# Transposed input in its own buffers, first weight blocks in halves, and the memory prepared earlier and partly on GpSimd, in a two-layer hybrid encoder

## The chip, the core and the metric

The kernel runs on one core of one Trainium2 chip. The metric is the device time of one execution in microseconds (us), the median of several runs. A core has TensorE (PE in the profile; its weight loads are PEld), VectorE (DVE), ScalarE (ACT), GpSimd (POOL) and SyncE (SP), which here only issues transfers. Each engine takes its instructions in a fixed order.

## What is computed

`DEPTH` = 2 layers act on `x` (256 frames of 1024 numbers, float32), with a memory `mem` of 256 rows of 1024:

```python
for l in range(DEPTH):
    h = rms_norm(x, ffn1_norms[l, 0])
    x = x + 0.5 * rms_norm(swiglu(h, ffn1_w13[l], ffn1_w2[l]), ffn1_norms[l, 1])
    h = rms_norm(x, mix_norms[l, 0])
    x = x + rms_norm(token_mixing(h, ...), mix_norms[l, 1])     # retention, latent attention, differential attention, gated and summed
    h = rms_norm(x, cross_norms[l, 0])
    m = rms_norm(mem, cross_norms[l, 2])
    x = x + rms_norm(cross_attention(h, m, cross_wq[l], cross_wkv[l], cross_wo[l]), cross_norms[l, 1])
    h = rms_norm(x, ffn2_norms[l, 0])
    x = x + 0.5 * rms_norm(swiglu(h, ffn2_w13[l], ffn2_w2[l]), ffn2_norms[l, 1])
```

## The kernel before

**Products in three passes.** Each float32 operand of a large product is split into a high part (written in the matmul format by ACT) and a low part (the rest, by DVE); a product is three matmuls, high by high, high by low and low by high. A weight block is [128 x 1024] float32 (512 KB). `load` brings it into one of 4 `raw` buffers with a transfer on SP's queue, then `split` writes `wh` (ACT, L170) and `wl` (DVE, L171), of which there are 8 each. A block serves both halves `i` of the 256 frames, 12 matmuls in all.

**The start.** While the first data come in, 14 matmuls on zeros run (L145). `first_chunk` then computes four weight blocks against the transposed input. Its piece (half `i` of the frames, half `h` of the 1024 rows) is loaded into a work buffer `xg` (two buffers in turn, L253, on SP's queue), multiplied by a gain (DVE, L254) and split into `xTh` and `xTl`. The first two weight blocks are loaded and split in halves, the others whole. The plain `x` and its mean squares follow.

**The mixer of a layer.** Three token mixers run one after the other; `weave` takes one step of each of its generators in turn, so that projections and gates (`fill`) stand between the short, dependent steps of attention. The last attention is `differential`: scores, softmax (DVE L892, L559, ACT L561, DVE L898 to L902), transposes on PE (L910), values (L920), and a norm of each head through POOL (L923, L680, L682, L156, L157, L925) and DVE (L927). Then `branches(2, ...)` and the output projection follow, in `finish`.

**The memory.** `memory` loads the transposed memory `mT` in two pieces into `raw` buffers, and makes of each of its 8 rows of tiles a scaled high part (ACT, L173) and low part (DVE, L174) in `mem`; it is woven with `branches(2, ...)`. In layer 0 it also loads the plain memory `m` in two pieces into `raw` buffers, for the mean square (ACT, L164) and the reciprocal root (POOL), kept in `rmem` (L954) for both layers. `cross` reads `mem` and `rmem`.

**Order.** The program is written in Python order, and a scheduler at compile time places each instruction in the queue of its engine; an instruction that comes late in the program can stand earlier in its queue where its engine has nothing else. So the transfer of `positions`, which the program names after 22 weight blocks, is issued behind the ninth block. `rope_tables`, called in the first feed-forward of layer 0 after its second chunk, makes the tables of the rotations.

Of the kernel before, what the change touches and what calls it, by code (L numbers as in the profile page):

```python
# [11 lines left out]
F32 = mybir.dt.float32  # L12
# [3 lines left out]
AF = mybir.ActivationFunctionType  # L16
ALU = mybir.AluOpType
# [3 lines left out]
P = 128  # L21
D = 1024
KD = D // P
SEQ = 256
NT = SEQ // P
# [86 lines left out]
def hybrid_encoder(ctx: ExitStack, tc: tile.TileContext, stream: Stream, t: dict, out: bass.AP):  # L112
    nc = tc.nc
# [3 lines left out]
    wp = ctx.enter_context(tc.tile_pool(name="wp", bufs=WP_BUFS))  # L117
# [35 lines left out]
    def rsq(ss, n=1, eps=EPS, c=1.0):  # L153

        a, b = stat(n), stat(n)
        nc.gpsimd.tensor_scalar(out=a, in0=ss, scalar1=eps, scalar2=c, op0=ALU.add, op1=ALU.mult)  # L156
        nc.gpsimd.tensor_tensor(out=b, in0=a, in1=mhalf[:, :n], op=ALU.pow)  # L157
        return b
# [8 lines left out]
    def split(h, l, src, scale=None):  # L167

        if scale is None:
            nc.scalar.activation(h, src, AF.Copy)  # L170
            nc.vector.tensor_tensor(out=l, in0=src, in1=h.bitcast(F32), op=ALU.subtract)  # L171
        else:
            nc.scalar.activation(h, src, AF.Copy, scale=scale)  # L173
            nc.vector.scalar_tensor_tensor(out=l, in0=src, scalar=scale, in1=h.bitcast(F32), op0=ALU.mult, op1=ALU.subtract)  # L174

    def load(blk, parts=1):

        blk = _freeze(blk)
        w = _blk_width(blk)
        off = stream.place(blk)  # L180
        raw = wp.tile([P, w], F32, tag="raw", name="raw", padded_shape=[P, BLK])
        h = hp.tile([P, w], F32R, tag="wh", name="wh", padded_shape=[P, BLK])
        l = hp.tile([P, w], F32R, tag="wl", name="wl", padded_shape=[P, BLK])
        for n in range(parts):
            c = slice(n * w // parts, (n + 1) * w // parts)
            nc.sync.dma_start(out=raw[:, c], in_=ws[off:off + P * w].rearrange("(p e) -> p e", p=P)[:, c])
            split(h[:, c], l[:, c], raw[:, c])
        nk = blk[3]
        return (h.rearrange("p (k n) -> p k n", k=nk), l.rearrange("p (k n) -> p k n", k=nk))
# [13 lines left out]
    def weave(*gens, fill=None):  # L203

        gens = list(gens)
        while gens:
            if fill is not None:
                next(fill, None)
            gens = [g for g in gens if next(g, gens) is not gens]
# [34 lines left out]
            nc.tensor.matmul(o, lhsT=aT[1][:, j0 + k, :], rhs=bh, start=False, stop=j0 + k == total - 1)  # L244
        tick()

    def first_chunk(blks, use):

        def scaled(i, h):

            k = slice(4 * h, 4 * h + 4)
            xg = wk.tile([P, 4, P], F32, tag="xg", name="xg")
            nc.sync.dma_start(out=xg, in_=t["xT"][:, i, k, :])  # L253
            nc.vector.tensor_tensor(out=xg, in0=xg, in1=gain0[:, k].unsqueeze(2).to_broadcast([P, 4, P]), op=ALU.mult)  # L254
            split(xT[i][0][:, k, :], xT[i][1][:, k, :], xg)

        def low(n):
            for i in range(NT):
                for k in range(2):
                    nc.tensor.matmul(o[i], lhsT=xT[i][1][:, 2 * n + k, :], rhs=tiles[n][0][:, k, :], start=False, stop=n == len(blks) - 1 and k == 1)  # L260

        o, tiles, r = [ps_tile() for _ in range(NT)], [], []
        for n, blk in enumerate(blks):
            if n % 2 == 0:
                scaled(0, n // 2)
            tiles.append(load(blk, 2 if n < 2 else 1))
            if n % 2 == 0:
                scaled(1, n // 2)
            for i in range(NT):
                for k in range(2):  # L270
                    mm2(o[i], xT[i][0][:, 2 * n + k, :], tiles[n][0][:, k, :], tiles[n][1][:, k, :], n == 0 and k == 0)
            if n:
                low(n - 1)
        for i in range(NT):
            nc.sync.dma_start(out=x[i], in_=t["x"][i * P:(i + 1) * P, :])
            r.append(rsq(mean_sq(x[i], D)))
        nc.sync.dma_start(out=ident, in_=t["c_ident"])
        low(len(blks) - 1)
        tick()
        for i in range(NT):  # L280
            use(i, o[i], r[i])
        return r
# [122 lines left out]
    def ffn(f, l, r, pg, ng, beside=lambda: None):  # L405
        b = _ffn_blocks(f, l)
        with tc.tile_pool(name="ff", bufs=2) as ff:
# [38 lines left out]

            first = r is None
            if first:
                r = first_chunk(b["w13", 0], both)
            else:  # L450
                lead(b["w13", 0], lambda i, o: both(i, o, r[i]), b["g", 1], use_gate(1))
            accs = new_accs()
# [26 lines left out]

    cs = const.tile([P, NT, 2, ROPE_W], F32, name="cs")  # L480

    def rope_tables():
        with tc.tile_pool(name="rt", bufs=1) as rt:
            n = ROPE_W // 2
            pi = rt.tile([P, NT], I32, name="pi")
            nc.sync.dma_start(out=pi, in_=t["positions"].rearrange("(t p) -> p t", p=P), allow_slow_non_contiguous=True)
# [84 lines left out]
    def mixer(l, r, pg, ng):  # L571
        with ExitStack() as es:
# [93 lines left out]
            def branches(b, y):  # L666
                return chain(branch(b, 0, y), branch(b, 1, y))
# [207 lines left out]
            def differential():  # L875
                steps = []
                for i in range(NT):
                    c = {}
                    steps += [[lambda i=i, c=c, g=g, fn=fn: fn(i, c, g) for fn in (dscores, dprobs, dvalues)] for g in range(2)]
                    steps[-1].append(lambda i=i, c=c: into_T(y_diff[i], 0, c["y"], 4))  # L880
                yield from skew(steps)
# [45 lines left out]
                    nc.vector.tensor_tensor(out=heads(c["y"], P), in0=heads(op, P), in1=f2.unsqueeze(2).to_broadcast([P, DIFF_H, P]), op=ALU.mult)  # L927

            mem = [xp.tile([P, KD, SEQ], F32R, tag=f"big{n}", name="mem") for n in range(2)]
            weave(differential(), fill=fill)  # L930
            weave(chain(fill, branches(2, y_diff)), memory(l, mem))

            work = [(xT, n, k) for n, k in enumerate(_rows("w_out", (l,), 8))]
            return finish(new_accs(), work, pg, ng, 1.0, True), mem
# [2 lines left out]
    def memory(l, mem):  # L937

        g = stat(KD)
        nc.sync.dma_start(out=g, in_=t["mgain"][l])  # L940
        for h in range(2):
            m = wp.tile([P, 4, SEQ], F32, tag="raw", name="mT")
            nc.sync.dma_start(out=m, in_=t["memT"][:, 4 * h:4 * h + 4, :])
            for k in range(4):
                mh, ml = (d[:, 4 * h + k, :] for d in mem)
                gk = g[:, 4 * h + k:4 * h + k + 1]
                split(mh, ml, m[:, k, :], gk)
                if k % 2:
                    yield
        if l == 0:  # L950
            for i in range(NT):
                m = wp.tile([P, D], F32, tag="raw", name="m")
                nc.sync.dma_start(out=m, in_=t["mem"][i * P:(i + 1) * P, :])
                nc.gpsimd.tensor_copy(out=rmem[:, i:i + 1], in_=rsq(mean_sq(m, D)))  # L954

    def cross(l, r, mem, pg, ng):
        with ExitStack() as es:
            cp = es.enter_context(tc.tile_pool(name="cp", bufs=2))
# [71 lines left out]
    r = None  # L1030
    for l in range(DEPTH):
        g = {k: t[f"{k}_norms"][l] for k in ("ffn1", "mix", "cross", "ffn2")}
        r = ffn("ffn1", l, r, g["ffn1"][1], g["mix"][0], *((rope_tables,) if l == 0 else ()))
        r, mem = mixer(l, r, g["mix"][1], g["cross"][0])
        r = cross(l, r, mem, g["cross"][1], g["ffn2"][0])
        r = ffn("ffn2", l, r, g["ffn2"][1], t["ffn1_norms"][l + 1, 0] if l + 1 < DEPTH else None)
# [64 lines left out]
```

## Time and profile before

| | us |
|---|---|
| median of 3 runs | 1456.21 (1455.73 to 1457.08) |
| the profiled execution, its own time | 1453.58 |
| span of its instructions | 1451.8 |
| PE busy | 1432.7 |
| DVE busy | 921.8 |
| ACT busy | 754.7 |
| POOL busy | 90.8 |

The span runs from the first to the last instruction of the profiled execution; its own time is 1.8 us longer. Busy time is the time in which an engine had at least one instruction under way. PE's share is 99%, so any change can win only where PE waits or runs at a lower clock. In the timeline a row gives start, length, engine, line, operation, output and inputs, count, and in brackets the idle time before it and what ended it; an engine with a q is its queue issuing a transfer.

### The profile page before, as it was taken

The numbers are of one execution on the slowest core, as the hardware profiler recorded it, in microseconds if no ns is written. First come the engines' busy times: TensorE is split into PE (matmuls) and PEld (weight loads), VectorE is DVE, ScalarE is ACT, GpSimd is POOL, SyncE is SP. The second block draws the span as 40 slices with busy tenths as digits, with TensorE's granted clock in tenths as the row PEclk, the third lists the DMA queues.
The fourth block names the chain that finished last, engine by engine and source line by source line (L and its number), as shares of the span: only waits on it lengthen the run. The fifth ranks groups of instructions, "written<-read, shape, count | busy, mean of one in ns | idle before, by whom it ended". The sixth has DMA issues, their size and how long they took to land.

```text
span 1451.8 us, 18502 instructions
## 1 busy us (share of the span) xinstructions
PE 1432.7 (99%) x6778; PEld 1189.6 (82%) x6778; DVE 921.8 (63%) x1209; ACT 754.7 (52%) x1102; POOL 90.8 (6%) x190
## 2 busy tenths in 40 slices
PE   8999999999999999999999999999999999999998
PEld 6888888888778888888888888888887788888886
DVE  5776576566767556665576555865667765665554
ACT  5444455654556646454464544666555565554442
POOL 0000022100201001000000000221001010000000
PEclk9999999999999999999999999999999999999999
DMA  8777756454466437777577765655444574476672
GB/s 277 245 259 262 241 183 207 153 160 141 154 201 217 155 127 229 257 237 232 190 224 246 249 227 199 208 175 186 145 155 145 163 239 145 140 258 226 218 227 92
DMA packets 109020, 290.14 MB, mean 200 GB/s; under 512 B 14909, under 2 KB 38397, under 8 KB 108925
## 3 DMA queue, kind: packets, MB, share of 16 engines
q1 hardware_dynamic: 76528, 265.89, 55.9%
q10 hardware_dynamic: 32400, 23.08, 4.9%
q8 instruction: 53, 0.87, 0.3%
q14 instruction: 39, 0.31, 0.1%
HBM read 276.34 MB, written 12.58 MB: 199 GB/s over the span
## 4 chain that ended last, share of the span: by engine, by line
PE 80%; DMA 8%; DVE 5%; ACT 3%; issue 2%; POOL 1%; SPq 0%; ACTq 0%; DVEq 0%; POOLq 0%
PE ps L226 25%; PE ps L227 25%; PE ps L231 24%; DMA gM<-far 4%; PE ps L312 2%; DMA raw<-in_ws 2%; DMA far<-gB 2%; DVE wl L171 2%; ACT wh L170 1%; PE ps L835 1%; PE ps L855 1%; PE ps L244 1%; POOL st L157 0%; DVE tg L657 0%; ACT junk L344 0%
## 5 line engine op out<-in xcount | busy, mean ns | idle before, releaser
L171 DVE TENSOR_TENSOR wl<-raw,wh 128x1024 fp32r<-128x1024 f32 (+1 forms) x480 | 575.0, 1213 | 206.7 <-ACT wh L170 198.1
L170 ACT ACTIVATE wh<-raw 128x1024 fp32r<-128x1024 f32 (+1 forms) x480 | 498.5, 1050 | 285.8 <-PE ps L231 185.0
L226 PE MATMUL ps<-wh,xTh 128*128 128x512 f32 (+1 forms) x1312 | 518.3, 395 | 4.9 <-ACT xTh L170 2.7
L227 PE MATMUL ps<-wl,xTh 128*128 128x512 f32 (+1 forms) x1312 | 510.6, 389 | 1.9 <-DVE wl L171 1.8
L231 PE MATMUL ps<-wh,xTl 128*128 128x512 f32 (+1 forms) x1256 | 488.9, 390 | 1.0 <-DVE xTl L174 0.9
L226 PEld LDWEIGHTS ps<-wh,xTh 128*128 128x128 f32 x1312 | 246.7, 188 | 57.9 <-ACT xTh L170 5.3
L227 PEld LDWEIGHTS ps<-wl,xTh 128*128 128x128 f32 x1312 | 246.9, 188 | 52.0 <-DVE wl L171 4.2
L231 PEld LDWEIGHTS ps<-wh,xTl 128*128 128x128 f32 x1256 | 235.8, 188 | 50.9 <-DVE xTl L174 1.8
L226 PE MATMUL ps<-wh,gTh 128*128 128x512 f32 x352 | 137.2, 390 | 0.0
L231 PE MATMUL ps<-wh,gTl 128*128 128x512 f32 x352 | 137.0, 389 | 0.0
L227 PE MATMUL ps<-wl,gTh 128*128 128x512 f32 x352 | 136.9, 389 | 0.0
L170 ACT ACTIVATE gTh<-gM 128x512 fp32r<-128x512 f32 (+1 forms) x48 | 28.6, 597 | 156.1 <-DMA gM<-far 156.1
L171 DVE TENSOR_TENSOR gTl<-gM,gTh 128x512 fp32r<-128x512 f32 (+1 forms) x48 | 31.0, 646 | 105.5 <-ACT gTh L170 105.5
L231 PEld LDWEIGHTS ps<-wh,gTl 128*128 128x128 f32 x352 | 66.1, 188 | 13.8
L227 PEld LDWEIGHTS ps<-wl,gTh 128*128 128x128 f32 x352 | 66.1, 188 | 13.7
L226 PEld LDWEIGHTS ps<-wh,gTh 128*128 128x128 f32 x352 | 66.1, 188 | 13.5
L350 POOL TENSOR_SCALAR st<-st 128x1 f32<-128x1 f32 x16 | 4.9, 306 | 941.2 <-ACT junk L344 941.2
L432 DVE SCALAR_TENSOR_TENSOR g<-ps,st,s 128x512 f32<-128x512 f32 (+1 forms) x48 | 33.7, 703 | 28.4 <-PE ps L231 28.4
L561 ACT ACTIVATE e<-ps,st 128x256 f32<-128x256 f32 (+1 forms) x80 | 33.6, 431 | 34.4 <-DVE st L559 34.3
L226 PE MATMUL ps<-wh,mem 128*128 128x512 f32 x128 | 51.0, 398 | 0.0
L231 PE MATMUL ps<-wh,mem 128*128 128x512 f32 x128 | 50.0, 390 | 0.0
L227 PE MATMUL ps<-wl,mem 128*128 128x512 f32 x128 | 49.9, 390 | 0.0
(203 smaller groups left out, 1279.2 us busy)
## 6 DMA issues: line engine op xcount, KB each, us to landing
raw<-in_ws SPq DMA_DIRECT2D x464, 512.0 KB, 4.5
far<-gB ACTq DMA_DIRECT2D x40, 256.0 KB, 2.3
gM<-far ACTq DMA_DIRECT2D x40, 256.0 KB, 4.6
gain<-in_ffn_norms SPq DMA_DIRECT2D x7, 512.0 KB, 5.4
raw<-in_ws SPq DMA_DIRECT2D x8, 416.0 KB, 5.2
gain<-in_mix_norms SPq DMA_DIRECT2D x4, 512.0 KB, 5.2
gain<-in_cross_norms SPq DMA_DIRECT2D x4, 512.0 KB, 5.3
mT<-in_memT SPq DMA_DIRECT2D x4, 512.0 KB, 3.5
```

The source lines that it names most:

```text
L170: nc.scalar.activation(h, src, AF.Copy)
L171: nc.vector.tensor_tensor(out=l, in0=src, in1=h.bitcast(F32), op=ALU.subtract)
L226: nc.tensor.matmul(o, lhsT=ah, rhs=bh, start=first, stop=False)
L227: nc.tensor.matmul(o, lhsT=ah, rhs=bl, start=False, stop=False)
L231: nc.tensor.matmul(o, lhsT=al, rhs=bh, start=False, stop=last)
L244: nc.tensor.matmul(o, lhsT=aT[1][:, j0 + k, :], rhs=bh, start=False, stop=j0 + k == total - 1)
L312: nc.tensor.transpose(p[:rows, i * P:(i + 1) * P], src[:, i * rows:(i + 1) * rows], ident)
L350: nc.gpsimd.tensor_scalar(out=a, in0=parts[0], scalar1=parts[1], scalar2=EPS * c, op0=ALU.add, op1=ALU.add)
L432: nc.vector.scalar_tensor_tensor(out=g[:, :w], in0=up, scalar=r, in1=s[:, :w], op0=ALU.mult, op1=ALU.mult)
L561: nc.scalar.activation(e[:, h, :w], s[:, j, :], AF.Exp, bias=nm[:, h:h + 1], accum_out=sums[:, h:h + 1])
L835: nc.tensor.matmul(s[h], lhsT=qT[i][:, 4 * g + h, :], rhs=kT[:, 4 * g + h, :w], start=True, stop=True)
L855: nc.tensor.matmul(op[:, cc], lhsT=c["pT", g][:, k, h * P:(h + 1) * P], rhs=mv[k][:, 4 * g + h, :], start=k == 0, stop=k == i)
```

## The change

Four edits. (1) The pieces of the transposed input get four buffers of their own, and their transfers are issued on ACT's queue, all at the start. (2) All four blocks of `first_chunk` are loaded and split in halves. (3) `memory` is woven with `differential` instead of with `branches(2, ...)`; the scaling and the subtraction go to POOL, and ACT makes a plain copy. (4) The mean squares of `mem` move out of `memory` into `rope_tables` (now `tables`), that is into the first feed-forward of layer 0, with a buffer of their own, one for both pieces.

```diff
-    def first_chunk(blks, use):
+    def first_chunk(blks, use, pool):
+
+        xs = [[pool.tile([P, 4, P], F32, name=f"xs{i}{h}") for h in range(2)] for i in range(NT)]
+        for h in range(2):
+            for i in range(NT):
+                nc.scalar.dma_start(out=xs[i][h], in_=t["xT"][:, i, 4 * h:4 * h + 4, :])
 
         def scaled(i, h):
 
             k = slice(4 * h, 4 * h + 4)
-            xg = wk.tile([P, 4, P], F32, tag="xg", name="xg")
-            nc.sync.dma_start(out=xg, in_=t["xT"][:, i, k, :])
+            xg = xs[i][h]
             nc.vector.tensor_tensor(out=xg, in0=xg, in1=gain0[:, k].unsqueeze(2).to_broadcast([P, 4, P]), op=ALU.mult)
             split(xT[i][0][:, k, :], xT[i][1][:, k, :], xg)
...
-            tiles.append(load(blk, 2 if n < 2 else 1))
+            tiles.append(load(blk, 2))
...
             if first:
-                r = first_chunk(b["w13", 0], both)
+                with tc.tile_pool(name="first", bufs=1) as pool:
+                    r = first_chunk(b["w13", 0], both, pool)
...
-    def rope_tables():
+    def tables():
+
         with tc.tile_pool(name="rt", bufs=1) as rt:
+            for i in range(NT):
+                m = rt.tile([P, D], F32, name="m")
+                nc.sync.dma_start(out=m, in_=t["mem"][i * P:(i + 1) * P, :])
+                nc.gpsimd.tensor_copy(out=rmem[:, i:i + 1], in_=rsq(mean_sq(m, D)))
             n = ROPE_W // 2
...
-            weave(differential(), fill=fill)
-            weave(chain(fill, branches(2, y_diff)), memory(l, mem))
+            weave(differential(), memory(l, mem), fill=fill)
+            weave(chain(fill, branches(2, y_diff)))
...
                 gk = g[:, 4 * h + k:4 * h + k + 1]
-                split(mh, ml, m[:, k, :], gk)
+                nc.gpsimd.tensor_scalar(out=m[:, k, :], in0=m[:, k, :], scalar1=gk, scalar2=None, op0=ALU.mult)
+                nc.scalar.activation(mh, m[:, k, :], AF.Copy)
+                nc.gpsimd.tensor_tensor(out=ml, in0=m[:, k, :], in1=mh.bitcast(F32), op=ALU.subtract)
                 if k % 2:
                     yield
-        if l == 0:
-            for i in range(NT):
-                m = wp.tile([P, D], F32, tag="raw", name="m")
-                nc.sync.dma_start(out=m, in_=t["mem"][i * P:(i + 1) * P, :])
-                nc.gpsimd.tensor_copy(out=rmem[:, i:i + 1], in_=rsq(mean_sq(m, D)))
...
-        r = ffn("ffn1", l, r, g["ffn1"][1], g["mix"][0], *((rope_tables,) if l == 0 else ()))
+        r = ffn("ffn1", l, r, g["ffn1"][1], g["mix"][0], *((tables,) if l == 0 else ()))
```

## Rows read from the trace of the kernel before

**Rows 1.** The page, busy time, share of the span and instructions of each engine.

```profile
PE 1432.7 (99%) x6778; PEld 1189.6 (82%) x6778; DVE 921.8 (63%) x1209; ACT 754.7 (52%) x1102; POOL 90.8 (6%) x190
```

**Rows 2.** Busy time by stretch: length, engines (instructions), granted clock, DMA share, GB/s.

```profile
7.00:23.00 16.00, 13.14 (x52) 9.16 (x51) 10.23 (x14) 9.51 (x16) 1.50 (x4) 1.00 0.84 305
34.00:40.00 6.00, 5.69 (x24) 4.10 (x23) 4.39 (x6) 5.67 (x8) 0.00 (x0) 1.00 0.58 194
410.00:415.00 5.00, 4.45 (x21) 3.13 (x20) 5.00 (x7) 3.76 (x5) 0.00 (x0) 1.00 0.68 218
415.00:420.00 5.00, 3.31 (x13) 2.16 (x13) 5.00 (x8) 2.51 (x3) 0.00 (x0) 0.92 0.66 213
420.00:425.00 5.00, 5.00 (x20) 3.90 (x20) 3.30 (x5) 1.55 (x2) 0.00 (x0) 0.74 0.79 260
1135.00:1140.00 5.00, 4.10 (x20) 3.07 (x20) 4.29 (x7) 1.66 (x2) 0.00 (x0) 1.00 0.64 198
```

**Rows 3.** Timeline of the start.

```profile
0.72 0.39 SPq L253 DMA_DIRECT2D xg<-in_xT  x1
1.16 1.28 ACT L140 ACT_TABLE_LOAD   x1 [1.16 <-PEq L1074]
4.84 0.69 DVE L254 TENSOR_TENSOR xg<-xg,st 128x512 f32<-128x512 f32 x1 [3.35 <-DMA st<-in_gain]
6.94 0.33 SPq L253 DMA_DIRECT2D xg<-in_xT  x1
6.95 0.40 PE L226 MATMUL ps<-wh,xTh 128*128 128x512 f32 x1
20.53 1.98 PE L260 MATMUL ps<-wh,xTl 128*128 128x512 f32 x8
22.34 0.62 PE L226 MATMUL ps<-wh,xTh 128*128 128x512 f32 x2
```

**Rows 4.** Tile xg in the first 40 us, its transfers' time from issue to landing.

```profile
DMA to landing us min/median/max: 3.9/4.3/4.7
```

**Rows 5.** Timeline of ACT from 386 us, where it turns from weights to the memory.

```profile
392.49 1.06 ACT L170 ACTIVATE wh<-raw 128x1024 fp32r<-128x1024 f32 x1 [0.40 <-DMA raw<-in_ws]
396.63 1.06 ACT L164 ACTIVATE junk<-m 128x1024 bf16<-128x1024 f32 x1 [3.08 <-DMA m<-in_mem]
402.97 1.05 ACT L170 ACTIVATE wh<-raw 128x1024 fp32r<-128x1024 f32 x1
```

**Rows 6.** Timeline of SP's queue in the same stretch.

```profile
388.85 0.33 SPq L186 DMA_DIRECT2D raw<-in_ws  x1
397.80 13.56 SPq L186 DMA_DIRECT2D raw<-in_ws  x7
```

**Rows 7.** Tile mT: ns min/median/max, first and last start in us, forms.

```profile
L173 ACT ACTIVATE mem<-mT,st x16: 493/501/509, 397.7 to 1119.2; 128x256 fp32r<-128x256 f32 x16
L174 DVE SCALAR_TENSOR_TENSOR mem<-mT,st,mem x16: 476/480/485, 398.2 to 1119.9; 128x256 fp32r<-128x256 f32 x16
```

**Rows 8.** Groups of POOL's instructions: count, busy us, mean ns, idle before.

```profile
L627 POOL TENSOR_SCALAR csr<-cs,st 128x224 f32<-128x224 f32 x4 | 3.5, 868 | 0.2
L809 POOL COPY rot<-kr 128x128 f32<-128x128 f32 x8 | 2.4, 294 | 34.2 <-DVE wl L171 17.8 <-PE ps L312 15.4 <-DVE rg L698 0.7
```

**Rows 9.** Tile rmem: ns min/median/max, first and last start in us.

```profile
L954 POOL COPY rmem<-st x2: 391/829/1267, 398.8 to 404.1; 128x1 f32<-128x1 f32 x2
```

**Rows 10.** Timeline of DVE in and behind the differential attention of layer 0.

```profile
379.44 0.69 DVE L927 TENSOR_TENSOR rot<-ps,st 128x512 f32<-128x512 f32 x1 [1.48 <-POOL st L925]
404.05 1.23 DVE L171 TENSOR_TENSOR wl<-raw,wh 128x1024 fp32r<-128x1024 f32 x1 [1.32 <-ACT wh L170]
```

**Rows 11.** Timeline of PE in the same attention.

```profile
374.47 0.60 PE L910 MATMUL ps<-ident,e 128*128 128x128 f32 x4
384.24 0.83 PE L910 MATMUL ps<-ident,e 128*128 128x128 f32 x4 [1.08 <-DVE e L902]
```

**Rows 12.** Timeline of ACT in the first feed-forward.

```profile
34.07 0.42 ACT L170 ACTIVATE gTh<-gM 128x256 fp32r<-128x256 f32 x1 [3.55 <-DMA gM<-far]
```

## The prediction

> **What bounds the kernel.** I read the busy times first. TensorE works 1432.7 of 1451.8 us [rows 1], so 19 us are idle in all, and a change that removes no matmul can win only those and what a lower clock costs. Then I read the busy time by stretch to find where the idle time lies. Three places touch the change. From 7 to 23 us TensorE works 13.14 of 16 us [rows 2]. From 410 to 425 us, where layer 0's mixer ends, it works 4.45, 3.31 and 5.00 us out of 5 each, and the granted clock is 0.92 and 0.74 in the last two [rows 2]. In layer 1 the same place, 1135 to 1140 us, has 0.90 us idle [rows 2].
>
> The timeline gives the causes. At the start, the third piece of the transposed x is issued only at 6.94 us, when the first work buffer has come free [rows 3]. The first matmul on data starts at 6.95 us and the next chunk's first at 22.34 us, so the first chunk takes 15.39 us [rows 3]. Its work is 4 blocks of 12 matmuls; 8 of them take 1.98 us and one alone 0.40 us [rows 3], so the pitch is (1.98 - 0.40)/7 = 0.226 us and 48 take 10.9 us. About 4.5 us are lost to waits, plus the wait for the first data.
>
> In the mixer of layer 0 the reader should look at ScalarE: it splits a weight block at 392.49 us and the next at 402.97 us [rows 5]. Between them it stands 3.08 us before the memory's mean square, whose data are late [rows 5], and does the memory's copies. SP issues no weight block from 388.85 to 397.80 us, since memory pieces hold the ring [rows 6]. TensorE lives on blocks split before that and runs out near 410 us. The loss is 0.55 + 1.69 us idle. For the clock: 0.92 and 0.74 are means of the two levels, 2.4 and 1.2 GHz, so 16% and 52% of 5 us each ran at half, 3.4 us, in which half the work was lost: 1.7 us. Together 3.9 us.
>
> **Edits 1 and 2, the start.** SP's queue loses four transfers and ScalarE's gains them, and the two-buffer wait goes. Before, the first piece was issued at 0.72 us, its transfers land after 3.9 to 4.7 us, and the multiplication started at 4.84 us, released by the gain's transfer [rows 3, 4]. Behind the gain's issue ScalarE's queue has a table load from 1.16 us that takes 1.28 us [rows 3]. If the queue runs ahead of it the piece is issued near 1.2 us; if it waits, near 2.5 us. It now also shares the DMA engines with weight halves that SP issues from 0.72 us. So the multiplication starts at 1.2 + 4.5 = 5.7 us as I take it, at best at the old 4.84 us, at worst at 2.6 + 4.7 = 7.3 us. From multiplication to first matmul took 6.95 - 4.84 = 2.1 us and stays. I take the first value, since the transfers need nothing that the table load makes; both ends stay in the range.
>
> Behind the first matmul come 10.9 us of matmuls. All four pieces and blocks are now on their way by about 5 us, and the halves let the last two blocks begin earlier, so I leave 0.8 us of waits. Next chunk: 5.7 + 2.1 + 10.9 + 0.8 = 19.5 us, a gain of 2.8 us. With 4.84 us and no waits it is 17.8 (gain 4.5); with 7.3 us and 0.8 us of waits 21.1 (gain 1.2). The splits cost no more engine time than before except a few instruction starts, hidden in VectorE's idle time, 5.8 of 16 us [rows 2]; without that cover they would cost some tenths.
>
> The Trainium skill, DMA: Bandwidth & Descriptors, section Issuing engines are not separate DMA queues, says that starting transfers on several engines saves only the sequencer's time, since all run on the same 16 DMA engines. By that rule the second queue gains nothing here beyond some issue time, and the own buffers alone are worth the 2.8 us. The rows agree as far as they go: what held the third piece was the buffer, not the queue.
>
> **Edit 4, mean squares in the first feed-forward.** Moved: two transfers of 512 KB on SP, two ScalarE squares of 1.06 us [rows 5] and their accumulator reads, six small POOL instructions. In place of two ring buffers there is one own buffer, so the second transfer holds SP until the first square is done. Behind it stand the weight blocks. They should take the place in SP's queue that the positions had, behind the ninth block. There the DMA engines are well filled (a share of 0.84 up to 23 us [rows 2]), and there is no reserve: ScalarE stands 3.55 us before a returning gated piece at 34.07 us, with weight splits queued behind it [rows 12], and TensorE loses 0.31 us from 34 to 40 us [rows 2]. A megabyte more there delays what follows. Lower bound nothing (the blocks split ahead cover it); upper bound the wait that this transfer itself caused at its old place, 3.08 us [rows 5]. I take 1.2 us, nearer the lower end, since only the first piece should fall into the tight stretch.
>
> **Edit 3, the end of the mixers.** In layer 0 the hole in the weight stream (388.85 to 397.80 us on SP, 392.49 to 402.97 us on ScalarE) goes. What layer 1 loses with the memory's copies alone, 0.9 us, is the most that should remain; I take 0.5 us remaining, so 3.4 us gained. Bounds 1 and 3.9 us. In layer 1 I take 0.5 us, bounds 0 and 0.9 us.
>
> **Edit 3, what the differential attention pays.** Removed are 8 VectorE operations of 0.48 us a layer; ScalarE keeps 8 of about 0.50 us [rows 7]. Added are 16 POOL operations a layer on 128x256. The trace has none of this width. From below: a copy of 128x128 takes 0.29 us; from above: a scaling of 128x224 takes 0.87 us [rows 8], so 0.87 x 256/224 = 1.0 us, and once more for a second input, 2.0 us. I take 1.0 us, an estimate from the wider row: 16 us a layer, in a stretch of about 40 us where POOL has almost nothing else. On top of it stands a contention that the trace shows: POOL's one-column copy takes 0.39 us alone and 1.27 us at 404.06 us [rows 9], where it started with a weight's low part on VectorE, which ran from 404.05 for 1.23 us [rows 10].
>
> The Trainium skill, SBUF — State Buffer, section SBUF: two separate sides, says why: VectorE with two SBUF inputs and GpSimd share a pair of ports that one of them holds for a whole instruction while the other fully blocks. The rule speaks against the edit, for POOL would hold up VectorE's splits too. By it the 16 us of POOL could all become waits of VectorE.
>
> No row shows VectorE held up by POOL's port, so a loss of none stays possible; but a delay by POOL's results is there: VectorE stands 1.48 us at 379.44 us for the norm's last POOL operation, and TensorE then 1.08 us at 384.24 us for the softmax [rows 10, 11]. This chain has no reserve. But over the span ScalarE is busy 52% and POOL 6% [rows 1], and the memory work is needed only in the cross attention, so most should run in gaps. I take 1.0 us more loss in each layer, 2.0 in all; bounds 0 and, as worked out in the rival below, 14 us.
>
> **The sum.** -2.8 + 1.2 - 3.4 - 0.5 + 2.0 = -3.5 us. The profiled execution's own time of 1453.58 us becomes 1450.1; the median of the runs is 1456.21 us, 2.6 above it, so the median should be 1452.7 us.
>
> **The rivals.** First, within 0.2% (2.9 us, about what this measurement can tell from no change). The start gives only 1.2 us because the pieces wait behind the table load, the memory's transfers cost 2 us, and the ends of the mixers give 3.9 less 2.0 in the attention. Sum -1.1, 1455.1 us. Here belongs too the case that the change does not do what it says: the scheduler places by its own estimates, the memory pieces still need ring buffers, and POOL's work slides back toward the mixer's end. For it: a transfer stands 13 blocks ahead of its place in the program already. Against it: POOL is nearly idle, so nothing keeps that work from going early.
>
> Second, slower. POOL becomes what the differential attention waits for. Its steps stand 384.24 - 374.47 = 9.8 us apart at the slowest [rows 11], some 7 us otherwise, and the memory adds 4 POOL operations to each of four steps. At 1.0 us and a wait of 1.22 us for a low-part split [rows 10] it is 8.9 us a step: POOL falls back by 1.9 us in each of four steps, 7 us a layer, and the norm's POOL operations queue behind. Two layers lose 14 us; with the start and the ends gained (2.8 - 1.2 + 3.9 = 5.5) the time is 1464.7 us. It decides from about 1.75 us for each POOL operation, waits included. By the port rule cited above this is the expected case if each operation meets a split.
>
> Third, much faster: 4.5 us at the start, 4.8 at the mixers' ends, nothing paid. 1456.2 - 9.3 = 1446.9 us.
>
> **Chances and range.** My forecast, a gain of 2.9 to 6 us, 0.46; much faster 0.08; within 0.2% 0.32; slower 0.14, as POOL is idle 94% of the span [rows 1] and the memory is needed late. So faster 0.54, same 0.32, slower 0.14. The range 1448.3 to 1458.5 us leaves out the slower case, the end of the much faster one and a little of the middle, about 2 in 10. The forecast's own range is 1450.2 to 1453.3 us.
>
> **What would show it.** In the changed profile: the first matmul on data near 7.8 us and the next chunk near 19.5 us; weight splits on ScalarE without a hole from 390 to 403 us; a full clock around 420 us; POOL operations on mT of about 1 us; and TensorE's waits at its transposes L910 longer by about 1 us in each layer. I am wrong if the first matmul comes after 9 us, if ScalarE stands before the moved mean square, or if POOL's operations take 2 us.

## The result: slower, and where the time went

| | before | after |
|---|---|---|
| median, us | 1456.12 (1455.73 to 1457.08, 4 runs) | 1469.05 (1468.31 to 1472.14, 4 runs) |
| the profiled execution, own time | 1453.58 | 1469.62 |
| span | 1451.8 | 1467.8 |

The ratio is 1.0092 (95% interval 1.0074 to 1.0109). The change costs 12.9 us; I had forecast a gain of 3.5. The profiled executions lie 16.0 us apart, since the one of before was 2.5 us under its median and the one of the changed kernel 0.6 us above its own. The ledger below accounts for these 16.0.

The page's busy times of the changed kernel answer to [rows 1]:

```profile
PE 1436.9 (98%) x6778; PEld 1190.9 (81%) x6778; DVE 920.5 (63%) x1195; ACT 754.6 (51%) x1104; POOL 117.2 (8%) x222
```

TensorE has 30.9 us without work where it had 19.1. POOL has 26 us more work and DVE hardly less. To find the place I took marks that both kernels have. These are TensorE's in the timeline of the changed kernel: the end of layer 0's first feed-forward, then for each layer the first scores of the differential attention, the first transpose of `z` behind it, and the first matmul on `mem` in the cross attention.

```profile
194.48 0.38 PE L316 MATMUL ps<-ident,xg 128*128 128x128 f32 x2
356.52 0.38 PE L899 MATMUL ps<-dkT,dqT 64*128 64x128 f32 x2
423.62 0.27 PE L316 MATMUL ps<-ident,z 128*128 128x128 f32 x1
450.93 0.48 PE L226 MATMUL ps<-wh,mem 128*128 128x512 f32 x1
1080.92 0.38 PE L899 MATMUL ps<-dkT,dqT 64*128 64x128 f32 x2
1147.29 0.27 PE L316 MATMUL ps<-ident,z 128*128 128x128 f32 x1
1174.57 0.48 PE L226 MATMUL ps<-wh,mem 128*128 128x512 f32 x1
```

Before, the same marks stood at 191.73, 353.86, 411.66, 442.99, 1072.79, 1130.04 and 1158.51 us; the two that bound layer 0's differential attention are these:

```profile
353.86 0.38 PE L889 MATMUL ps<-dkT,dqT 64*128 64x128 f32 x2
411.66 0.33 PE L312 MATMUL ps<-ident,z 128*128 128x128 f32 x1 [0.55 <-DVE z L658]
```

The differences, each less the one ahead of it, are: first feed-forward +2.7, differential attention of layer 0 +9.3, mixer's end -4.0, differential attention of layer 1 +9.1, mixer's end -1.2. The stretches between add 0.1. So the ends of the mixers gained a little more than forecast, and the two differential attentions lost 18.4 us.

The windows of the changed kernel (columns as in [rows 2]):

```profile
7.00:23.00 16.00, 13.62 (x54) 9.84 (x55) 13.29 (x19) 12.68 (x21) 2.06 (x4) 1.00 0.93 347
354.00:366.00 12.00, 12.00 (x64) 9.51 (x63) 8.26 (x17) 6.54 (x16) 3.29 (x4) 1.00 0.48 142
366.00:378.00 12.00, 5.61 (x26) 4.26 (x26) 5.70 (x7) 6.90 (x18) 10.50 (x15) 0.81 0.28 89
378.00:390.00 12.00, 11.13 (x50) 7.95 (x49) 11.48 (x21) 5.74 (x13) 3.15 (x6) 0.90 0.67 216
410.00:425.00 15.00, 15.00 (x71) 12.39 (x70) 11.05 (x13) 8.15 (x9) 0.00 (x0) 1.00 0.55 178
```

and two of the same windows of the kernel before:

```profile
366.00:378.00 12.00, 12.00 (x66) 9.47 (x65) 11.62 (x22) 6.15 (x13) 1.71 (x5) 1.00 0.50 162
378.00:390.00 12.00, 10.91 (x56) 8.91 (x55) 8.19 (x14) 5.88 (x13) 1.63 (x5) 1.00 0.18 56
```

Most of the loss lies in the 12 us from 366 us: TensorE works 5.61, VectorE 5.70, ScalarE 6.90, and only POOL is full, with 10.50. Before, TensorE worked all 12. The DMA share is 0.28 where it was 0.50: SP issues no weight block from 365.0 to 373.6 us. The granted clock is 0.81 and 0.90 there, that is, part of the stretch at 1.2 GHz. At the end of this mixer, where [rows 2] show the hole of before, TensorE now has no gap over 0.05 us up to the first matmul on `mem` at 450.93 us.

Here is the chain in layer 0, engine by engine, from the timeline of the changed kernel. First SP's queue:

```profile
330.42 0.33 SPq L953 DMA_DIRECT2D mT<-in_memT  x1
341.56 0.33 SPq L953 DMA_DIRECT2D mT<-in_memT  x1
358.04 0.42 SPq L950 DMA_DIRECT2D st<-in_mgain  x1
```

The scheduler fetched the two memory pieces long ahead, at 330 and 342 us; each lands 3.5 to 3.6 us after its issue. The gains that they are multiplied by, 4 KB, are fetched only at 358.04 us. POOL:

```profile
362.89 4.29 POOL L957 TENSOR_SCALAR mT<-mT,st 128x256 f32<-128x256 f32 x4 [2.46 <-DMA st<-in_mgain]
367.15 1.43 POOL L959 TENSOR_TENSOR mem<-mT,mem 128x256 fp32r<-128x256 f32 x2
```

So the layer's 16 operations begin only at 362.89 us, in the middle of the softmax. ScalarE:

```profile
363.86 0.42 ACT L958 ACTIVATE mem<-mT 128x256 fp32r<-128x256 f32 x1 [0.54 <-POOL mT L957]
369.52 0.42 ACT L958 ACTIVATE mem<-mT 128x256 fp32r<-128x256 f32 x1 [1.89 <-POOL mT L957]
370.74 0.35 ACT L571 ACTIVATE e<-ps,st 128x128 f32<-128x128 f32 x1
```

Its copies wait for POOL one by one, and the exponentials (L571), whose input VectorE had finished at 365.96 us, stand behind them in the same queue until 370.74 us. VectorE and TensorE:

```profile
365.22 0.74 DVE L569 TENSOR_REDUCE st<-ps 128x2 f32<-128x256 f32 x2
372.26 0.18 DVE L908 RECIPROCAL st<-st 128x4 f32<-128x4 f32 x1 [6.30 <-ACT e L571]
373.21 3.44 DVE L912 SCALAR_TENSOR_TENSOR e<-e,st 128x128 f32<-128x128 f32 x2
```

```profile
369.26 0.60 PE L930 MATMUL ps<-dv,pT 128*128 128x128 f32 x4
375.24 0.45 PE L920 MATMUL ps<-ident,e 128*128 128x128 f32 x1 [5.37 <-ACT wh L170]
376.70 0.48 PE L920 MATMUL ps<-ident,e 128*128 128x128 f32 x1 [1.02 <-DVE e L912]
```

VectorE idles 6.30 us for the exponentials; then its two operations L912, which took 0.61 us in the kernel before (there L902), take 3.44 us beside POOL's subtractions. TensorE idles 5.37 and 1.02 us. (The first wait is put down to ScalarE's weight copy, which ended at about the same time; the transposes read what L912 writes, and the first of its two operations ended at 375.09 us.) Idle time in the two windows from 366 us grew from 1.09 to 7.26 us, that is by 6.2; the other 3.1 of the 9.3 us are put down, by difference, to the matmuls at the lower clock of these windows.

In the first feed-forward SP's queue and VectorE show the second loss:

```profile
28.21 0.42 SPq L492 DMA_DIRECT2D m<-in_mem  x1
44.06 0.42 SPq L492 DMA_DIRECT2D m<-in_mem  x1
60.78 0.42 SPq L500 DMA_DIRECT2D inv<-in_c_inv  x1
```

```profile
67.22 0.25 DVE L503 TENSOR_SCALAR ang<-inv,pf 128x56 f32<-128x56 f32 x1 [5.63 <-DMA inv<-in_c_inv]
```

The two memory transfers took the places that the positions and `inv` had (22.98 and 47.66 us before). `inv` now comes 13 us later, VectorE stands 5.63 us for it, where the kernel before has no such wait, and the low parts of weights stand behind. TensorE is without work for 3.2 us between 70 and 110 us, nearly all of it in waits for such low parts; before it was 0.6 us.

The start in the timeline answers to [rows 3]:

```profile
5.97 0.69 DVE L258 TENSOR_TENSOR xs<-xs,st 128x512 f32<-128x512 f32 x1 [4.49 <-DMA xs<-in_xT]
7.38 0.50 PE L226 MATMUL ps<-wh,xTh 128*128 128x512 f32 x1 [0.84 <-ACT xTh L170]
7.84 0.69 DVE L258 TENSOR_TENSOR xs<-xs,st 128x512 f32<-128x512 f32 x1 [1.17 <-DMA xs<-in_xT]
9.19 0.50 PE L227 MATMUL ps<-wl,xTh 128*128 128x512 f32 x1 [1.30 <-DVE wl L171]
14.41 1.06 ACT L164 ACTIVATE junk<-x 128x1024 bf16<-128x1024 f32 x1 [0.91 <-DMA x<-in_x]
16.86 0.61 ACT L170 ACTIVATE xTh<-xs 128x512 fp32r<-128x512 f32 x1
17.53 0.50 PE L226 MATMUL ps<-wh,xTh 128*128 128x512 f32 x1 [0.62 <-ACT xTh L170]
21.77 0.39 PE L226 MATMUL ps<-wh,xTh 128*128 128x512 f32 x1
```

The next chunk begins at 21.77 instead of 22.34 us: 0.6 us gained here, 1.3 us at the first `gTh` matmul (43.95 for 45.27 us).

### The profile page after: what moved, and what is told of

It reads as the page before. It is cut to its first block, busy times and chain, and to the rows that moved or that the text cites. A ratio compares the mean times of both kernels' runs of the same rounds, so it can differ in the third digit from the quotient of the medians.

```text
span 1467.8 us, 18522 instructions
## 1 busy us (share of the span) xinstructions
PE 1436.9 (98%) x6778; PEld 1190.9 (81%) x6778; DVE 920.5 (63%) x1195; ACT 754.6 (51%) x1104; POOL 117.2 (8%) x222
## 4 chain that ended last, share of the span: by engine, by line
PE 83%; DMA 6%; DVE 5%; ACT 2%; POOL 2%; issue 2%; SPq 0%; ACTq 0%; POOLq 0%; DVEq 0%
PE ps L226 26%; PE ps L227 26%; PE ps L231 25%; PE ps L316 3%; DMA gM<-far 2%; DMA far<-gB 2%; DVE wl L171 1%; ACT wh L170 1%; PE ps L845 1%; PE ps L865 1%; POOL mT L957 1%; PE ps L244 1%; POOL st L157 1%; DMA x<-in_x 0%; DMA inv<-in_c_inv 0%
## 5 line engine op out<-in xcount | busy, mean ns | idle before, releaser
L171 DVE TENSOR_TENSOR wl<-raw,wh 128x1024 fp32r<-128x1024 f32 (+2 forms) x482 | 575.3, 1208 | 225.7 <-ACT wh L170 217.1
L170 ACT ACTIVATE wh<-raw 128x1024 fp32r<-128x1024 f32 (+2 forms) x482 | 498.8, 1046 | 309.4 <-PE ps L231 181.7
L171 DVE TENSOR_TENSOR gTl<-gM,gTh 128x512 fp32r<-128x512 f32 (+1 forms) x48 | 30.9, 643 | 92.1 <-ACT gTh L170 91.8
L571 ACT ACTIVATE e<-ps,st 128x256 f32<-128x256 f32 (+1 forms) x80 | 33.5, 431 | 30.6 <-DVE st L569 30.6
```

Of the source, the lines that this page charges most:

```text
L571: nc.scalar.activation(e[:, h, :w], s[:, j, :], AF.Exp, bias=nm[:, h:h + 1], accum_out=sums[:, h:h + 1])
```

## The experiments

The edits below are shortened; "..." stands for what is left out. The theories: A, ScalarE's copies wait for POOL and the exponentials behind them; B, the early place is too full; C, POOL's operations slow VectorE's where both read SBUF; D, the memory pieces hold two of the four ring buffers and stop the weights; E, the late gains decide; F, `inv` is displaced in SP's queue; G, the megabyte and its squares cost by themselves. A "layer" below is the change of the differential attention's length between the marks, layer 0 / layer 1, in us, and "end" that of the mixer's end; these are of one profile each, which can lie some us off the median (e8's is the slowest of its ten runs, 4.9 us above). Ratios are to before on the same chip, whose median was 1453.95 to 1456.39 us.

| run | median us | ratio (95%) | first FFN | layer | end |
|---|---|---|---|---|---|
| changed kernel | 1469.05 | 1.0092 (1.0074 to 1.0109) | +2.7 | +9.3 / +9.1 | -4.0 / -1.2 |
| e1_early_split | 1462.24 | 1.0049 (1.0028 to 1.0070) | +6.7 | +5.1 / +4.9 | -4.1 / -1.2 |
| e5_act_first | 1482.85 | 1.0182 (1.0158 to 1.0207) | -0.4 | +15.6 / +15.6 | -4.0 / -1.2 |
| e3_norms_behind_tables | 1464.54 | 1.0062 (1.0042 to 1.0082) | -3.0 | +9.6 / +9.7 | -4.0 / -1.2 |
| e4_start_alone | 1450.14 | 0.9970 (0.9951 to 0.9989) | -0.8 | -0.7 / -0.1 | -2.1 / +0.2 |
| e7_own_buffers | 1476.14 | 1.0152 (1.0123 to 1.0182) | +0.6 | +12.2 / +12.7 | -4.1 / -1.1 |
| e8_split_own_buffers | 1455.08 | 1.0008 (0.9993 to 1.0023) | +2.2 | +4.2 / +4.8 | -4.0 / -1.2 |
| e9_act_first_own | 1463.05 | 1.0063 (1.0038 to 1.0089) | +0.1 | +6.0 / +6.3 | -4.1 / -1.2 |
| e10_start_and_norms | 1446.65 | 0.9946 (0.9931 to 0.9961) | -4.0 | -0.7 / +0.1 | -2.7 / 0.0 |
| e14_pool_alone | 1452.93 | 0.9974 (0.9962 to 0.9987) | -2.2 | +2.3 / +3.2 | -3.0 / -0.3 |
| e12_pool_late | 1461.56 | 1.0038 (1.0020 to 1.0057) | -3.7 | +5.5 / +5.5 | -1.5 / +1.5 |
| e11_best_own | 1445.54 | 0.9922 (0.9907 to 0.9937) | -2.5 | -0.3 / +0.3 | -4.0 / -0.8 |
| e6_gains_early | 1451.30 | 0.9959 (0.9945 to 0.9973) | +0.1 | +0.9 / +1.7 | -4.0 / -1.2 |
| e15_gain_own_tile | 1453.11 | 0.9982 (0.9965 to 1.0000) | +2.3 | +1.2 / +1.7 | -4.0 / -1.2 |
| e16_gains_and_norms | 1448.64 | 0.9950 (0.9931 to 0.9970) | -2.6 | +0.9 / +1.9 | -4.0 / -1.1 |
| e17_gains_norms_split | 1445.41 | 0.9935 (0.9915 to 0.9955) | -3.0 | -0.3 / +0.4 | -4.1 / -1.2 |

**POOL or the place.** e1 keeps the early place but lets ScalarE and VectorE split the memory; e5 keeps POOL's 16 operations but lets ScalarE make the high part from the unscaled piece, ahead of POOL.

```diff
 e1
-nc.gpsimd.tensor_scalar(...); nc.scalar.activation(mh, m[:, k, :], AF.Copy); nc.gpsimd.tensor_tensor(...)
+split(mh, ml, m[:, k, :], gk)
 e5
+nc.scalar.activation(mh, m[:, k, :], AF.Copy, scale=gk)
 nc.gpsimd.tensor_scalar(out=m[:, k, :], in0=m[:, k, :], scalar1=gk, ...)
-nc.scalar.activation(mh, m[:, k, :], AF.Copy)
```

> The changed kernel, but the memory's high and low parts are made as before by ScalarE and VectorE; the place (beside the differential attention) stays. Theory A (ScalarE's copies wait for GpSimd's scaling, and the softmax's exponentials stand behind them in ScalarE's queue): the 9 us lost in the differential attention of each layer fall to 1 or 2 us, the time to about 1456 (the kernel before, within 2 us), and the first transposes L920 of each layer's second head group wait under 1 us. Theory B (the place itself is too full, whoever does the work): the waits stay near 5 us in each layer and the time near 1469 us. Theory C (GpSimd's reads lock VectorE out): as A, since GpSimd's reads are gone.

> The changed kernel, but ScalarE makes the scaled high part straight from the loaded piece, ahead of GpSimd's scaling; GpSimd still does all of its 16 operations a layer. ScalarE then waits for no GpSimd result, while the port is used as much as before. Theory A: the differential attention of each layer loses some 3 us instead of 9, the time is about 1457 us. Theory C (the port): still 9 us in each layer and two updates of e by VectorE of 1.6 to 1.9 us each, the time 1468 us. Theory B: 1469 us.

e1 lies between the theories: POOL accounts for 4 us of each layer, 5 remain without it, with the gains as late as in the changed kernel. e5 missed every expectation. The first stall shrank to 0.4 us, as A says, but in the next group TensorE and ScalarE read:

```profile
386.84 0.69 PE L920 MATMUL ps<-ident,e 128*128 128x128 f32 x2 [12.31 <-DVE e L912]
```

```profile
381.46 1.06 ACT L170 ACTIVATE wh<-raw 128x1024 fp32r<-128x1024 f32 x1 [7.14 <-DMA raw<-in_ws]
382.42 0.46 ACT L571 ACTIVATE e<-ps,st 128x256 f32<-128x256 f32 x1
```

ScalarE waits for a weight transfer, with the exponentials behind it. SP could not issue that transfer: it stands from 369.94 to 377.88 us for POOL's subtractions, which hold the memory pieces' ring buffers. That gave theory D.

**Own buffers.** e7, e8 and e9 are the changed kernel, e1 and e5 with the pieces in scratch of the rotations that is idle in this stage.

```diff
-m = wp.tile([P, 4, SEQ], F32, tag="raw", name="mT")
+ms = [big(f"tmp{j}").rearrange("p (k t) -> p k t", k=2) for j in "ab"]
```

> The changed kernel, but the 2 MB of scaled memory land in four tiles of the rotation scratch, which nothing uses in this stage, instead of in two of the four buffers of the weight ring; operations, engines and place are those of the changed kernel (two transfers of 256 KB stand for one of 512 KB). Theory A (ScalarE's copies wait for GpSimd's scaling, and the exponentials are queued behind the copies): nothing changes, each differential attention still loses 9 us, 1467 to 1471 us. Theory D (the memory pieces keep two weight buffers until GpSimd is done with them, and the weight stream stands still): the stall ahead of the first transposes (4.5 to 5.4 us) stays, what comes behind it shrinks, 5 to 6 us in each layer, 1460 to 1464 us. Had D been all of it, 1 us in each layer, 1454 us.

> As the run with the split by ScalarE and VectorE in the early place, which took 1462.2 us and lost 5 us in each differential attention, but with the memory pieces in the rotation scratch instead of the weight ring. Theory B (the place has no room on ScalarE and VectorE for eight copies and eight subtractions): the same again, 1460 to 1464 us. Theory D (the weight ring): the 5 us become 0 to 2 us, 1452 to 1457 us.

> As the run in which ScalarE makes the high part from the unscaled piece ahead of GpSimd's two operations, which took 1482.9 us with a stall of 12.3 us in each layer, but with the memory pieces in the rotation scratch. Theory D: the stall of 12.3 us is gone, what is left in a layer is 1 to 4 us (VectorE slowed beside GpSimd's operations), 1453 to 1461 us. If the stall has another cause (VectorE and GpSimd getting in each other's way by itself), it stays: above 1475 us.

D is right for e5: the stall of 12.31 us becomes 3.61 in e9 and the layer falls from 15.6 to 6.0, more than the 1 to 4 expected to be left. For the changed kernel it is refuted: e7 is slower by 2.9 and 3.5 us a layer. The wait of theory A is still there: VectorE stands 5.79 us for the exponentials, with all eight of ScalarE's copies ahead of them instead of six. Behind them a weight stands in VectorE's queue between the steps of the softmax, and beside POOL another of its operations takes 2.68 instead of 0.68 us:

```profile
371.00 2.68 DVE L668 TENSOR_TENSOR z<-z,tg 128x512 f32<-128x512 f32 x1
373.73 1.21 DVE L171 TENSOR_TENSOR wl<-raw,wh 128x1024 fp32r<-128x1024 f32 x1
```

In e8 the layer moved by 0.2 to 1.0 us only, against D. Its median, 1455.08 us, lies where D put it and 7 us under e1's, but not for D's reason: of the 5.65 us between the two profiles the marks put 4.6 into the first feed-forward, where every engine's instructions stand in the same order in both.

**POOL's operations alone, and late.** e10 is before with the start edits and the mean squares behind the tables. e14 adds to it 16 POOL operations that nobody reads; e12 is e10 with the memory by POOL, in the old place.

```diff
 e14, against e10
+nc.gpsimd.tensor_scalar(out=d[0], in0=flat, scalar1=first[0], scalar2=None, op0=ALU.mult)   # 8 a layer
+nc.gpsimd.tensor_tensor(out=d[1], in0=flat, in1=d[0], op=ALU.subtract)                      # 8 a layer
-weave(differential(), fill=fill)
+weave(differential(), idle_pool(), fill=fill)
 e12, against the changed kernel with edit 4 moved as in e3
-weave(differential(), memory(l, mem), fill=fill)
-weave(chain(fill, branches(2, y_diff)))
+weave(differential(), fill=fill)
+weave(chain(fill, branches(2, y_diff)), memory(l, mem))
```

> The version of 1446.65 us (both start edits, mean squares behind the rope tables, memory in its old place by ScalarE and VectorE), plus, in each layer's differential attention behind the first softmax, 16 GpSimd operations of the shapes of the changed kernel's (8 scalings, 8 subtractions, 128x256) from a constant table into scratch that nobody reads. Every other engine's instructions stand in the same order as without them. So nothing waits for GpSimd, and only its use of the memory ports can cost. Theory C (GpSimd's operations hold up VectorE's operations with two inputs): 1 to 4 us in each layer, 1449 to 1455 us, and some of VectorE's operations take 1 to 3 us where they took 0.4 to 1.2. Theory A (only the waiting in the queues counts): 1446 to 1448 us.

> Both start edits, mean squares behind the rope tables, scaling and subtraction of memory by GpSimd as in the changed kernel, but in the old place beside the second half of the branches. If the place is what costs (no softmax queues behind ScalarE's copies there), 1446 to 1449 us, as with the split by ScalarE and VectorE in that place (1446.65). If GpSimd costs in any place, because weight splits wait behind ScalarE's copies or VectorE's subtractions are held up: 2 to 5 us in each layer, 1451 to 1457 us.

e14 loses 3.0 and 3.1 us a layer against e10, with the order of every other engine's instructions unchanged: C is right, with its size. Two rows of e14,

```profile
364.05 1.75 DVE L171 TENSOR_TENSOR wl<-raw,wh 128x1024 fp32r<-128x1024 f32 x1
378.43 0.69 DVE L939 TENSOR_TENSOR rot<-ps,st 128x512 f32<-128x512 f32 x1 [2.04 <-POOL st L937]
```

and the same two of e10,

```profile
362.46 1.23 DVE L171 TENSOR_TENSOR wl<-raw,wh 128x1024 fp32r<-128x1024 f32 x1 [0.31 <-ACT wh L170]
375.31 0.69 DVE L937 TENSOR_TENSOR rot<-ps,st 128x512 f32<-128x512 f32 x1 [1.47 <-POOL st L935]
```

show a split stretched by 0.52 us, and the norm, which the expectation overlooked: its POOL operations stand behind the 16, and VectorE waits 2.04 for 1.47 us. TensorE's idle time in layer 0's attention grows by 1.3 of the 3.0 us; the granted clock, 1.00 throughout in e10, is 0.86 in the 12 us around the longer wait. So the 3 us hold the stretched operations, the queue and the lower clock. e12 shows that POOL costs in the old place too, 6.1 and 5.5 us a layer more than e10, and its time lies above the range expected for that. TensorE waits 5.95 us until 413.27 us for `z`, behind ScalarE's copies, which wait for POOL one by one, and the weight splits behind them: theory A's wait at another place, with weights in place of exponentials. The place is not what costs there.

**The gains.** In all runs so far with the early place the gains came late. e6 loads them once in the first feed-forward; e15 changes nothing but the buffer they go to.

```diff
 e15
-g = stat(KD)                 # one of 48 small buffers that all statistics use in turn
+g = mgains[l]                # a tile of its own; the transfer stays on this line
 nc.sync.dma_start(out=g, in_=t["mgain"][l])
```

> The changed kernel, with the memory's gains loaded once in the first FFN, so that GpSimd's first scaling need not wait for them (it started 2.5 us after it could have). Theory A: all of GpSimd's results and ScalarE's copies come 2.5 us earlier, the stalls of 5.4 and 4.6 us ahead of the transposes shrink to 2 to 3 us, 1462 to 1466 us. If the stalls come from GpSimd's hold on VectorE's operations or from the ring: 1467 to 1471 us.

> The changed kernel, with the memory's gains (4 KB) loaded at the same place of the program, but into a tile of their own instead of one of the 48 small buffers that all statistics use in turn. Theory E (the changed kernel is slow because this small transfer waits for its buffer until the first softmax, so that memory pieces that landed 13 to 29 us earlier keep their ring buffers and all 16 GpSimd operations fall into the differential attention): its transfer goes out long before, GpSimd works ahead of the differential attention, 1450 to 1454 us, as with the gains loaded in the first FFN (1451.3). If loading them in the first FFN helped for another reason, the place in the program being late: 1467 to 1471 us.

e6 was far better than any theory then held: 17.8 us under the changed kernel with the same 16 operations. e15 names the cause. With a tile of its own the transfer goes out at 84.6 us instead of 358.04, and POOL's work goes by itself to the latent attention ahead, where all of it is done by 352.7 us, before the first scores of the differential attention:

```profile
333.83 3.64 POOL L958 TENSOR_SCALAR mT<-mT,mgain 128x256 f32<-128x256 f32 x4 [43.65 <-DMA mT<-in_memT]
346.32 3.63 POOL L958 TENSOR_SCALAR mT<-mT,mgain 128x256 f32<-128x256 f32 x4 [5.11 <-DMA mT<-in_memT]
```

The layers cost 1.2 and 1.7 us, near the 1.0 of the forecast, though no memory work is left in that attention; where these come from is not shown.

**The first feed-forward, and both repairs.** e3 puts edit 4 behind the work on the rope tables, e4 leaves edits 3 and 4 out, e11 is e10 with own buffers, e16 the changed kernel with both repairs, e17 e16 with the split of e1.

```diff
 e3
-for i in range(NT): m = rt.tile(...); dma m; rmem[:, i] = rsq(mean_sq(m, D))     # ahead of the positions
 ... positions, inv, angles, cs ...
+for i in range(NT): m = rt.tile(...); dma m; rmem[:, i] = rsq(mean_sq(m, D))     # behind them
```

> The changed kernel, but inside the moved helper the memory's loads and mean squares stand behind the rotation tables instead of ahead of them. Theory F (the two memory transfers took the places of the positions and of the frequencies in SP's queue, so that VectorE stood 5.6 us for the frequencies): the first feed-forward loses at most 1 us against the kernel before instead of 4.1, the time falls by about 3 us to 1466 us. Rival G (the megabyte itself, or ScalarE's two squares, cost it): the loss stays 4 us, the time 1469 us.

> The kernel before with the first two edits alone: own buffers for the transposed x from ScalarE's queue, and all four first blocks in halves. The changed kernel's trace has its first gated piece on TensorE 1.3 us earlier than before. If that gain is the start's own and is kept, the time is 1455 us, 1.3 us under the kernel before. If the predicted 2.8 us were there and eaten by the memory's transfers, 1453.3 us. If later stages absorb it, 1456 us.

> The two edits at the start and the mean squares of memory in the first FFN, but behind the rope tables' work; scaling of memory in its old place by ScalarE and VectorE. Theory F (the megabyte and the squares cost the first FFN nothing once they stand behind inv in the queue): 1446 to 1450 us, at or under the 1450.1 us of the two edits alone. Theory G (they cost by themselves): 1451 to 1454 us.

> The version of 1446.65 us, with the scaled memory's pieces in the rotation scratch instead of two buffers of the weight ring. Theory D at the old place: the ring's buffers are free for weights, the remaining stalls at the ends of the mixers (0.5 to 1.5 us a layer) go, 1444 to 1446 us. If the ring is not short there: 1446 to 1448 us, no difference.

> The changed kernel with both repairs: gains in own tiles, loaded with the mean squares behind the rope tables. Theories E and F together: the 3 to 4 us of the first FFN come on top of 1451.3, so 1446 to 1449 us. If the two overlap, 1449 to 1452 us.

> As the run with both repairs, but the memory split by ScalarE and VectorE, no GpSimd. Theory E: the early place was never too full, the 5 us a layer of the early split came from the late gains too; 1445 to 1449 us, within 2 us of the one with GpSimd. Theory B (eight copies and eight subtractions have no room ahead of the cross attention's own stage): 1452 to 1458 us.

F is right, and G is not. In e3 the two memory transfers are issued at nearly the same times as in the changed kernel (28.21 and 44.06 us), but `inv` ahead of them, and VectorE does not wait for it:

```profile
32.31 0.42 SPq L496 DMA_DIRECT2D inv<-in_c_inv  x1
35.99 0.42 SPq L553 DMA_DIRECT2D m<-in_mem  x1
41.97 0.37 SPq L553 DMA_DIRECT2D m<-in_mem  x1
38.46 0.40 DVE L499 TENSOR_SCALAR ang<-inv,pf 128x56 f32<-128x56 f32 x2
```

In all eight kernels with the squares ahead of the tables VectorE stands 2.5 to 5.6 us for `inv`, and TensorE is idle for 1.0 to 5.9 us between 70 and 110 us. In the seven with them behind, neither happens. Single profiles scatter in the length of this stage: the eight kernels with the squares ahead of the tables end this stage at -0.4 to +6.7 us, mean +1.8; the seven with them behind at -4.0 to -2.2, mean -3.0. The groups don't overlap. e16 shows that the two repairs add up (0.9950): its ten runs all lie under the ten of e15, by 4.5 us at the median. In e17, with the gains there in time, ScalarE and VectorE do the memory's work for -0.3 and +0.4 us a layer, against 4.9 to 5.1 in e1. So B falls for the place in the program; but in e17 the work runs by 340 us, ahead of the differential attention. Where it fell into that attention without POOL (e1, e8) it cost 4 to 5 us. e10, e11 and e17, 1445.4 to 1446.7 us, are the fastest and not told apart; all leave POOL out of the memory, which costs 3 us where it stays (e16 for e17). e4 missed all three of its expectations: it gained 3.8 us on its chip, more than the most hopeful of them.

## Why the prediction was wrong, by its steps

**Start, forecast -2.8, measured -0.6: right in direction, mis-sized.** Multiplication at 5.97 us (5.7 forecast) and first matmul at 7.38 (7.8) were right; the term of 0.8 us of waits behind it was not. From 7.38 to 21.77 us are 14.39 us, less the 10.9 us of matmuls 3.5 us. The longest gap is the 1.30 us ahead of 9.19 us: the low part of the first weight stands in VectorE's queue behind the second piece, whose data are late. The fourth piece's high part comes at 16.86 us, behind two mean squares of `x` on ScalarE that themselves wait for data. I had counted all transfers on their way by about 5 us; SP issued the last half of a weight block at 8.02 us. The DMA share is 0.93 where it was 0.84 [rows 2], and the fourth piece's transfer took 5.6 us where these pieces took 3.9 to 4.7 [rows 4]. This fits the Trainium skill, DMA: Bandwidth & Descriptors, section Issuing engines are not separate DMA queues, by which all run on the same DMA engines whoever starts them; no run here separates the second queue from the own buffers.

**Mean squares, forecast +1.2: right sign, other cause.** The changed kernel stands 3.5 us behind e4 at the end of this stage. The sum had the megabyte itself as the cost. It is what the megabyte displaced: put behind the tables, at nearly the same time, it costs nothing. I had written that the transfers take the positions' place and did not ask what came with the positions.

**Mixers' ends, forecast -3.4 and -0.5: right**, -4.0 and -1.2, both just past their bounds of 3.9 and 0.9. In layer 0 that is in part luck: e4, which leaves the memory's work as it was, gains 2.1 us there. Its waits behind the first transpose of `z` add up to 1.5 us, those of before to 1.7, but its granted clock is 1.00 over the next 15 us where before it was 0.89. So nearly the same waits cost the lower clock in one execution and not in the other, and the 1.7 us of clock in the forecast are not the edit's alone.

**The differential attention, forecast +1.0 a layer: this step failed**, with +9.3 and +9.1. Its sentence "the memory work is needed only in the cross attention, so most should run in gaps" asked when the result is needed, and not when the inputs are there. POOL's operations took 0.93 and 0.74 us by median, 13.3 us a layer, under the 16 estimated. But their first input, a 4 KB transfer that no term of the sum names, was tied by its buffer to a late place in SP's queue, in the first softmax (e15 moved it with the buffer alone; which release it waits for, no trace shows). It put 13 us of work, with ScalarE's copies and the exponentials behind them in one queue, on the chain without reserve. With the buffer changed the number would have been nearly right (1.2 and 1.7 us in e15), but the work then runs ahead of this attention, not in its gaps.

**The slower rival, 0.14, was right in place, and nearly in size** (14 us forecast, 18.4 measured), but not in cause, so that its nearness is luck. POOL did not fall behind by its rate; that needed 1.75 us an operation, and it had 0.93. The norm's POOL operations did queue behind, for 0.6 us in e14.

**The contention, left at nothing or all**, is at most 3 us a layer by e14, the norm's queue and the lower clock included. It shows on both sides: POOL's 16 operations, 13.3 us by their medians in the changed kernel, take 20.5 us there, and VectorE's take some tenths longer each, up to 2.0 us in e7. Now rows agree with the rule of the Trainium skill, SBUF — State Buffer, section SBUF: two separate sides, that I had cited: the engine without the port waits (the split of 1.75 us for 1.23 in e14).

Open: why the clock fell at the end of layer 0's mixer before and not in e4; what the 1.2 and 1.7 us of e15 are; and what sets the scatter of the first feed-forward. None was tried.

## What to carry to other kernels

When work is moved, list for each of its inputs where its transfer is issued and which buffer it waits for; the smallest one can set the time. A result that is needed late can still do harm early: an engine's queue is in order, so a waiting instruction holds up all that stands behind it, here the softmax. When a transfer moves ahead in a queue, look at what loses that place.

## What I had not expected of the hardware

A POOL subtraction with two inputs of 128x256 took 0.736 us, less than the scaling with one (0.928 us). Beside POOL's operations VectorE's two operations on 128x128 took 1.88 and 1.63 us instead of about 0.35, and one on 128x512 2.68 instead of 0.68 us. That is more than any one POOL subtraction beside them: each ended 0.15 to 0.54 us after the last of two or three in a row. Behind idle time of 6.4 us another 3.1 us went, by difference, at the lower clock.
